# Column vectors loaded as rows, first weights from two queues, two-pass end of the layer norm, softmax sums over two accumulators

## The chip, the core and the metric

The kernel runs on one core of a Trainium2 chip. The metric is the device time of one execution in microseconds (us). TensorE is called PE here, VectorE DVE, ScalarE ACT, GpSimd POOL and SyncE SP, as in the profile.

## The reference

Two layers (D = 1024, 2048 positions, batch 1, float32). Each layer takes shift, scale and gate from `c @ w_ada[l] + b_ada[l]`, normalizes and modulates x, projects it, and runs three mixers on parts of the projection; the merge ends in a second layer norm:

```python
mod = c @ w_ada[l] + b_ada[l]
shift, scale, gate = jnp.split(mod, 3, axis=-1)
h = _layer_norm(x, LN_EPS) * (1.0 + scale[:, None, :]) + shift[:, None, :]
proj = h @ w_in[l]
q, k, v, g_a, cu, cb, cc, g_c, fu, g_f = jnp.split(proj, split_idx, axis=-1)
...
y_attn = _attention(q, k, v) * jax.nn.silu(g_a)
y_conv = cb * _short_conv(cc * cu, conv_w[l]) * jax.nn.silu(g_c)
y_four = _fourier(fu, f_mix[l]) * jax.nn.silu(g_f)
y = jnp.concatenate([y_attn, y_conv, y_four], axis=-1) @ w_out[l]
x = _layer_norm(DEEPNORM_ALPHA * x + (1.0 + gate[:, None, :]) * y, LN_EPS) * ln_g[l] + ln_b[l]
```

Attention has 8 query heads of 64 channels over 2 key heads, softmax over all 2048 positions.

## The kernel before

**Start.** `setup` makes constants and loads c as a tile of 128 partitions x 8 (L96), element by element. `h_norm` loads four tiles of x (L229). `mod_start` (L138) loads b_ada as 128 x 24 in the same manner. `mod_first` (L147, L149) streams eight 256 KB blocks of w_ada for one group of 512 outputs and multiplies them with c on PE; this runs for scale and shift before the first projection. `load_w` (L277) brings blocks of w_in. All loads are issued by SP in program order.

**Attention.** A unit is one chunk of 512 queries and one pair of heads; there are 16 per layer. A unit has four groups (b = 0 to 3) of four key tiles of 128. A group runs, on PE in the order "SSMSMSMM": S is `scores` for one key tile (L903, four terms for two heads into two psA banks), M is `row_max` for a later unit (L829, two matmuls into two psA banks, which DVE reduces at L832). ACT takes the exponential of the scores at L905 into a tile with both heads, tag XA for even key tiles and WL for odd ones, four buffers of each. At the end of the group `weigh` (L916) multiplies the four tiles of the group before with V. The tag psA has seven PSUM banks. At b = 2 `sums` of the unit before comes first (L953): matmuls with ones add up its softmax weights over the keys, four small ones per accumulator, all into one psA bank; ACT copies it (L956). A transposition (L842) and a DVE cast (L844) for the guard rows stand in some groups.

The softmax weights of 16 key tiles are first added up tile by tile. POOL adds most of them at once after the exponential (L938, one add per head); DVE adds four of them after they have been weighed (L935, both heads in one). Which ones is a table:

```python
DVE_KT = (2, 6, 10, 13), range(NKT)
```

The second entry is for the layer's last unit, where DVE adds alone. The first add of an accumulator needs two tiles, so the first tile is held until the second is there. After the last weighing of a unit `add_both` (L944) adds DVE's accumulator to POOL's, on POOL, and `sums` sees one accumulator. In the last unit there is no merge; `sums` runs over the accumulator and two tiles left over. The order on the engines in this part is the order of the program. Fourier mixing runs as background work in the first units of each layer.

**Merge.** `out_proj` multiplies tiles of 128 positions with w_out (L1101 to L1103), DVE adds ALPHA times x (L1132), takes the statistics (L207, L210), POOL takes the reciprocal root (`rsqrt`, L123 and L124), and `finish` ends the layer norm: DVE subtracts the mean and scales (L1070, 1024 wide), DVE multiplies by ln_g (L1073, two halves), POOL adds ln_b (L1074, two halves), and the tile is stored (L1075). `finish` of a tile is issued after the statistics of the next. Between the layers the next layer's normalization and projection are mixed into the last chunk.

Of the kernel before, what the change touches and what calls it, by code (L numbers as in the profile page):

```python
# [10 lines left out]
ALU = mybir.AluOpType  # L11
AX = mybir.AxisListType

P = 128
D = 1024
S = 2048
DEPTH = 2
NB = D // P
HD = 64
CH = 512  # L20
NCH = S // CH
NKT = S // P
# [16 lines left out]
class Trunk:  # L39
# [34 lines left out]
    def setup(self):  # L74
        nc = self.nc
        eye = self.t("HS", [P, P])
        make_identity(nc, eye)
        self.identr = self.const("identr", [P, P], F32R)
        nc.vector.tensor_copy(self.identr, eye)
        self.ident = self.identr.bitcast(F32)  # L80
        self.mhalf = self.const("mhalf", [P, 8])
        nc.gpsimd.memset(self.mhalf, -0.5)
        self.ones = self.const("ones", [P, 32])
        nc.gpsimd.memset(self.ones, 1.0)
        sel = self.t("HS", [P, P])
        nc.gpsimd.memset(sel, 0.0)
        for h in range(2):
            nc.gpsimd.memset(sel[h * HD:h * HD + 1, :], 1.0)
        self.sel = self.const("sel", [P, P], F32R)
        nc.vector.tensor_copy(self.sel, sel)  # L90
        alt = self.const("alt", [P, 2])
        nc.gpsimd.memset(alt[:, 0:1], 1.0)
        nc.gpsimd.memset(alt[:, 1:2], -1.0)
        self.alt = alt.unsqueeze(1).to_broadcast([P, CH // 2, 2])
        self.cT = self.const("cT", [P, NB])
        nc.sync.dma_start(self.cT, self.c[0].rearrange("(b p) -> p b", p=P))  # L96

        self.crep = self.t("TAB", [P, NB, 32])
        nc.vector.tensor_copy(self.crep, self.cT.unsqueeze(2).to_broadcast([P, NB, 32]))

        self.q1 = [self.dram(f"q1_{c}", [P, NPAIR, 2, CH]) for c in range(NCH)]
        self.ga = [[self.dram(f"ga{b}_{c}", [P, CH]) for c in range(NCH)] for b in range(4)]
        self.gf = [[self.dram(f"gf{b}_{c}", [P, CH]) for c in range(NCH)] for b in range(2)]
        self.us = [[self.dram(f"us{b}_{c}", [P, CH]) for c in range(HALF_CH)] for b in range(2)]
        self.fd = [[self.dram(f"fd{b}_{k}", [P, CH]) for k in range(4)] for b in range(2)]
        self.dft = self.dram("dft", [4, 4, 2, P, CH])
        self.yc = [[self.dram(f"yc{b}_{c}", [P, CH]) for c in range(NCH)] for b in range(2)]
        self.yf = [[self.dram(f"yf{b}_{c}", [P, CH]) for c in range(NCH)] for b in range(2)]
        self.gd = [self.dram(f"gd{l}", [D]) for l in range(DEPTH)]
        self.rs_dram = [self.dram(f"rs{i}", [2 * CH]) for i in range(2)]  # L110
        self.rc_dram = [self.dram(f"rc{i}", [2 * CH]) for i in range(2)]
        self.mods = {}
        self.bg = []
        self.gq = []
        self.beside = []
        self.later = []
        self.fu_u = {}
        self.sp2 = {}
        self.x1 = [self.dram(f"x1_{s}", [P, D]) for s in range(NKT)]

    def rsqrt(self, out, var, scale, eps, n):
        nc = self.nc
        nc.gpsimd.tensor_scalar(out, var, scale, eps, ALU.mult, ALU.add)  # L123
        nc.gpsimd.tensor_tensor(out, out, self.mhalf[:, 0:n], ALU.pow)  # L124
# [9 lines left out]

    def mod_start(self, l):
        nc = self.nc
        self.mods[l] = mod = self.small("mod", [P, 3 * NB], bufs=2)
        nc.sync.dma_start(mod, self.b_ada[l].rearrange("(b p) -> p b", p=P))  # L138
        nc.vector.tensor_scalar(mod[:, NB:], mod[:, NB:], 1.0, None, ALU.add)

    def mod_first(self, g, tag="H"):

        nc = self.nc
        ps = self.p("A", (P, P))
        for b in range(NB):
            w = self.t(tag, [P, CH])
            nc.sync.dma_start(w, self.w_ada[0, b * P:(b + 1) * P, g * CH:(g + 1) * CH])  # L147
            for j in range(4):
                nc.tensor.matmul(ps[32 * j:32 * j + 32, :], self.crep[:, b, :], w[:, j * P:(j + 1) * P],  # L149
                                 start=(b == 0), stop=(b == NB - 1))  # L150
        self.mod_add(0, g, self.mod_rows(ps))
# [733 lines left out]
            except StopIteration:  # L885
                self.bg.pop(0)

    DVE_KT = (2, 6, 10, 13), range(NKT)

    def scores(self, u, kt):  # L890
        nc = self.nc
# [27 lines left out]
    def add(self, u, kt, pt, w):  # L919
# [16 lines left out]
        else:  # L936
            for h in range(2):
                self.nc.gpsimd.tensor_tensor(acc[w][:, h], a[:, h], pt[:, h], ALU.add)  # L938

    def add_both(self, u):  # L940

        a, d = u["acc"]["p"], u["acc"].pop("d")
        for h in range(2):
            self.nc.gpsimd.tensor_tensor(a[:, h], a[:, h], d[:, h], ALU.add)  # L944

    def sums(self, u):

# [35 lines left out]
    def attention(self, l):  # L983
        self.yat = {}
        n = len(self.units)
        for g in range((n + 2) * self.NBT):
            ui, b = divmod(g, self.NBT)
            u = self.units[ui] if ui < n else None
# [18 lines left out]
            if 0 < g <= n * self.NBT:  # L1007
                v, c = divmod(g - 1, self.NBT)
                for j in range(self.BATCH):
                    self.weigh(self.units[v], self.BATCH * c + j)  # L1010
                if c == self.NBT - 1 and v < n - 1:
                    self.add_both(self.units[v])
            if u and b == 2:
                u["ga"] = self.t("EV", [P, CH])
                self.nc.sync.dma_start(u["ga"], self.ga[u["pr"]][u["ch"]])
# [37 lines left out]
    def out_proj(self, l):  # L1053
        nc = self.nc
        lnp = {}
# [10 lines left out]
        trans = late = iter(())  # L1066
        tail = []

        def finish(si, xt, mv, rs):
            nc.vector.tensor_scalar(xt, xt, mv[:, 0:1], rs, ALU.subtract, ALU.mult)  # L1070
            for m in range(2):
                xm = xt[:, m * CH:(m + 1) * CH]
                nc.vector.tensor_tensor(xm, xm, lnp["g", m], ALU.mult)  # L1073
                nc.gpsimd.tensor_tensor(xm, xm, lnp["b", m], ALU.add)  # L1074
            nc.sync.dma_start(self.out[0, si * P:(si + 1) * P, :] if l == DEPTH - 1 else self.x1[si], xt)  # L1075

        for ch in range(NCH):
            ys = [self.yat[r, ch] for r in range(4)]
# [12 lines left out]
            for s in range(4):  # L1091
                si = ch * 4 + s
                xt = self.t("XA", [P, D])
# [17 lines left out]
            for n in ((1, 0) if last else (0, 1)):  # L1111
# [9 lines left out]
                for s in range(4):  # L1121
                    si = ch * 4 + s
                    xt = xts[s]
                    if ch:
                        ps = self.p("A")
# [3 lines left out]
                    else:  # L1129
                        ps = pss[s]  # L1130
                    xn = xt[:, n * CH:(n + 1) * CH]
                    nc.vector.scalar_tensor_tensor(xn, xn, ALPHA, ps, ALU.mult, ALU.add)  # L1132
                    if (n == 0) == last:
                        mv = self.small("bmv", [P, 2])
                        rs = self.small("brs", [P, 1])
                        self.row_stats(mv, [xt[:, 0:CH], xt[:, CH:]])
                        self.rsqrt(rs, mv[:, 1:2], 1.0, LN_EPS, 1)
                        if tail:
                            finish(*tail.pop())
                        tail.append((si, xt, mv, rs))  # L1140
                    if last and n:
                        next(trans, None)
                        next(trans, None)
# [2 lines left out]
            if last:  # L1146
                finish(*tail.pop())
# [4 lines left out]
    def run(self, layers=DEPTH):  # L1152
# [1 line left out]
        self.setup()  # L1154
        xs = self.h_norm(0, 0)
        self.mod_start(0)
        self.mod_first(2)
        self.mod_first(0)
        w_fu = self.load_w(0, COL_FU, 0)
        h0 = [], []  # L1160
        self.chan_first(h0, self.h_trans_steps(0, xs, *h0), w_fu, self.spill(self.us, AF.Copy),
# [2 lines left out]
        w = self.load_w(0, COL_KV, P)  # L1164
# [78 lines left out]
```

## Time and profile before

| | us |
|---|---|
| three runs | 2670.92, 2672.66, 2678.76 |
| median | 2672.66 |
| profiled execution, its own time | 2675.07 |
| span of its instructions | 2673.2 |
| PE busy | 2623.7 |
| DVE busy | 1791.0 |
| POOL busy | 1191.6 |
| ACT busy | 904.5 |

The profile is of one execution, the one of 2675.07 us; its trace starts at 0 and ends at 2673.2. The mean clock granted to PE was 0.994 of full speed. Matmuls are pipelined and their ends are modelled, so PE's busy time is an upper view, and starts are more exact than ends.

### The profile page before, as it was taken

What the parts mean: (1) busy time and instruction counts of PE and PEld (TensorE: products, weight loads), DVE (VectorE), ACT (ScalarE), POOL (GpSimd) and SP (SyncE); (2) the same over time, 40 slices, a digit from 0 to 9 for tenths busy, and PEclk for the clock granted to TensorE, in tenths of its full rate; (3) what the DMA queues carried; (4) which work ended last, traced back from release to release, by engine and by line L of the source; (5) the groups of instructions that cost most, each with busy time, mean ns of one, the idle gap of its engine ahead of it and who ended that gap; (6) DMA issues with size and microseconds to landing.
All of it is one profiled execution on the core that took longest, in us unless ns stands there. A gap on an engine that the chain in (4) does not pass through costs nothing.

```text
span 2673.2 us, 39706 instructions
## 1 busy us (share of the span) xinstructions
PE 2623.7 (98%) x14820; PEld 1838.7 (69%) x14820; DVE 1791.0 (67%) x3053; ACT 904.5 (34%) x1789; POOL 1191.6 (45%) x989
## 2 busy tenths in 40 slices
PE   7999999999999999999999999999999999999998
PEld 5888888765555555568888888887655555555786
DVE  6754773457778877787885347535577877787755
ACT  3321521134444454530232125211444445445200
POOL 1200020046789888814231001100677898887134
PEclk9999999999999999999999999999999999999999
DMA  9753462322211111045445222522322110111432
GB/s 303 231 166 107 133 184 71 106 96 83 92 53 60 41 41 37 21 140 180 140 138 173 52 99 72 162 78 76 110 95 77 57 56 30 32 37 45 147 114 95
DMA packets 198673, 269.11 MB, mean 101 GB/s; under 512 B 38352, under 2 KB 109392, under 8 KB 197968
## 3 DMA queue, kind: packets, MB, share of 16 engines
q1 hardware_dynamic: 198480, 266.58, 31.3%
q8 instruction: 116, 1.90, 0.3%
q14 instruction: 77, 0.63, 0.1%
HBM read 205.29 MB, written 69.48 MB: 103 GB/s over the span
## 4 chain that ended last, share of the span: by engine, by line
PE 91%; DVE 4%; DMA 2%; issue 1%; POOL 1%; ACT 1%; SPq 0%; POOLq 0%; DVEq 0%; ACTq 0%
PE psA L903 19%; PE psC L916 16%; PE psA L372 9%; PE psA L373 9%; PE psA L374 9%; PE psA L829 5%; PE psA L1101 4%; PE psA L1103 4%; PE psA L1102 4%; PE psA L320 2%; PE psA L322 2%; PE psA L321 2%; DVE mx L832 1%; PE psA L953 1%; PE psA L749 1%
## 5 line engine op out<-in xcount | busy, mean ns | idle before, releaser
L832 DVE TENSOR_REDUCE mx<-psA 128x1 f32<-128x512 f32 x1024 | 634.0, 682 | 216.5 <-PE psA L829 215.4
L938 POOL TENSOR_TENSOR WH<-WH,WL 128x512 f32<-128x512 f32 x360 | 488.4, 1383 | 44.3 <-ACT WL L905 44.2
L903 PE MATMUL psA<-TAB,KK 64*128 64x512 f32 x3072 | 471.7, 409 | 5.7 <-DVE HS L844 5.4
L905 ACT ACTIVATE XA<-psA 128x512 f32<-128x512 f32 x512 | 278.7, 598 | 448.4 <-PE psA L903 326.9
L372 PE MATMUL psA<-H,WH 128*128 128x512 f32 x1008 | 399.1, 396 | 0.0
L373 PE MATMUL psA<-H,WH 128*128 128x512 f32 x1008 | 393.6, 390 | 0.0
L374 PE MATMUL psA<-H,WL 128*128 128x512 f32 x1008 | 392.9, 390 | 0.0
L903 PEld LDWEIGHTS psA<-TAB,KK 64*128 64x128 f32 x3072 | 274.7, 185 | 143.6 <-issue 51.1
L938 POOL TENSOR_TENSOR WH<-WH,XA 128x512 f32<-128x512 f32 x240 | 306.9, 1305 | 57.5 <-ACT XA L905 57.5
L905 ACT ACTIVATE WL<-psA 128x512 f32<-128x512 f32 x512 | 279.8, 606 | 23.1 <-PE psA L903 21.2
L916 PE MATMUL psC<-XA,V 128*64 128x512 f32 x1024 | 270.3, 606 | 0.0
L938 POOL TENSOR_TENSOR WH<-XA,WL 128x512 f32<-128x512 f32 x60 | 76.0, 1287 | 426.2 <-DVE mx L832 376.3
L916 PE MATMUL psC<-WL,V 128*64 128x512 f32 x1024 | 263.1, 592 | 0.0
L132 DVE TENSOR_TENSOR WL<-WR,WH 128x512 fp32r<-128x512 f32 (+2 forms) x240 | 113.3, 508 | 164.4 <-ACT WH L129 163.8
L372 PEld LDWEIGHTS psA<-H,WH 128*128 128x128 f32 x1008 | 189.2, 188 | 48.5 <-issue 9.3
L374 PEld LDWEIGHTS psA<-H,WL 128*128 128x128 f32 x1008 | 189.2, 188 | 40.3
L829 PE MATMUL psA<-KK,TAB 64*128 64x512 f32 x1024 | 208.1, 403 | 8.0 <-DVE mx L832 5.7
L373 PEld LDWEIGHTS psA<-H,WH 128*128 128x128 f32 x1008 | 189.4, 188 | 37.1
L903 PE MATMUL psA<-QS,sel 64*128 64x512 f32 x1024 | 206.2, 390 | 0.0
L129 ACT ACTIVATE WH<-WR 128x512 fp32r<-128x512 f32 (+2 forms) x248 | 107.8, 487 | 261.7 <-PE psA L373 111.8
L916 PEld LDWEIGHTS psC<-WL,V 128*64 128x64 f32 x1024 | 73.6, 137 | 146.7 <-issue 146.7
L123 POOL TENSOR_SCALAR rq<-rq 128x8 f32<-128x8 f32 (+1 forms) x48 | 10.6, 220 | 321.0 <-DVE rq L432 279.3
(237 smaller groups left out, 4101.9 us busy)
## 6 DMA issues: line engine op xcount, KB each, us to landing
WR<-in_w_in SPq DMA_DIRECT2D x176, 256.0 KB
WR<-in_w_ada SPq DMA_DIRECT2D x64, 256.0 KB
q<-EV SPq DMA_DIRECT2D x64, 256.0 KB
TAB<-q SPq DMA_DIRECT2D x64, 256.0 KB
H<-dft SPq DMA_DIRECT2D x64, 256.0 KB
XA<-in_x SPq DMA_DIRECT2D x24, 512.0 KB
XA<-x SPq DMA_DIRECT2D x20, 512.0 KB
dft<-in_k_dft SPq DMA_DIRECT2D x32, 256.0 KB
```

What stands on the lines that cost most here:

```text
L129: nc.scalar.activation(hi, src, AF.Copy)
L132: (lo_eng or nc.vector).tensor_tensor(lo, src, hi.bitcast(F32), ALU.subtract)
L372: nc.tensor.matmul(ps, w1, hh[b], start=(b == 0), stop=False)
L373: nc.tensor.matmul(ps, w1, hl[b], start=False, stop=False)
L374: nc.tensor.matmul(ps, w2, hh[b], start=False, stop=(b == NB - 1))
L829: nc.tensor.matmul(pss[h], u["q"][0][r, s * P:(s + 1) * P], self.kk1[u["kv"]][kc][r], start=True, stop=True)
L832: nc.vector.tensor_reduce(out=u["mx"][h][:, s, kc:kc + 1], in_=pss[h], axis=AX.X, op=ALU.max)
L903: nc.tensor.matmul(pss[h], k[r], q[r], start=i == 0, stop=i == len(terms) - 1)
L905: nc.scalar.activation(pt[:, h, :], pss[h], AF.Exp, scale=HD ** -0.5)
L916: nc.tensor.matmul(u["pv"][h * HD:(h + 1) * HD, :], v, pt[:, h, :], start=(kt == 0), stop=(kt == NKT - 1))
L938: self.nc.gpsimd.tensor_tensor(acc[w][:, h], a[:, h], pt[:, h], ALU.add)
L1101: nc.tensor.matmul(ps, yh[:, sl], wh, start=first, stop=False)
```

## The change

`columns` loads c and b_ada as 8 and 24 rows of 128 elements, transposes them on PE and copies them from PSUM. `mod_first` can issue every second block of w_ada from ACT's queue; the first two groups do. DVE adds key tiles 3, 7, 11 and 15, `add_both` is gone, and `sums` runs over both accumulators. `finish` is split: `centre` computes (x - mean) * ln_g in one DVE pass per half, before the root is there, `finish` times the root plus ln_b in a second pass; the very last tile is stored in halves.

```diff
@@ -92,8 +92,7 @@
         nc.gpsimd.memset(alt[:, 0:1], 1.0)
         nc.gpsimd.memset(alt[:, 1:2], -1.0)
         self.alt = alt.unsqueeze(1).to_broadcast([P, CH // 2, 2])
-        self.cT = self.const("cT", [P, NB])
-        nc.sync.dma_start(self.cT, self.c[0].rearrange("(b p) -> p b", p=P))
+        self.cT = self.columns(self.const("cT", [P, NB]), self.c[0], nc.sync)
 
         self.crep = self.t("TAB", [P, NB, 32])
         nc.vector.tensor_copy(self.crep, self.cT.unsqueeze(2).to_broadcast([P, NB, 32]))
@@ -118,6 +117,17 @@
         self.sp2 = {}
         self.x1 = [self.dram(f"x1_{s}", [P, D]) for s in range(NKT)]
 
+    def columns(self, out, src, queue):
+
+        nc = self.nc
+        n = out.shape[1]
+        rows = self.t("HS", [n, P])
+        queue.dma_start(rows, src.rearrange("(b p) -> b p", p=P))
+        ps = self.p("A", (P, n))
+        nc.tensor.transpose(out=ps, in_=rows, identity=self.ident[0:n, 0:n])
+        nc.vector.tensor_copy(out, ps)
+        return out
+
     def rsqrt(self, out, var, scale, eps, n):
         nc = self.nc
         nc.gpsimd.tensor_scalar(out, var, scale, eps, ALU.mult, ALU.add)
@@ -134,17 +144,17 @@
 
     def mod_start(self, l):
         nc = self.nc
-        self.mods[l] = mod = self.small("mod", [P, 3 * NB], bufs=2)
-        nc.sync.dma_start(mod, self.b_ada[l].rearrange("(b p) -> p b", p=P))
+        self.mods[l] = mod = self.columns(self.small("mod", [P, 3 * NB], bufs=2), self.b_ada[l], nc.sync)
         nc.vector.tensor_scalar(mod[:, NB:], mod[:, NB:], 1.0, None, ALU.add)
 
-    def mod_first(self, g, tag="H"):
+    def mod_first(self, g, tag="H", queues=1):
 
         nc = self.nc
         ps = self.p("A", (P, P))
         for b in range(NB):
             w = self.t(tag, [P, CH])
-            nc.sync.dma_start(w, self.w_ada[0, b * P:(b + 1) * P, g * CH:(g + 1) * CH])
+            queue = nc.scalar if b % queues else nc.sync
+            queue.dma_start(w, self.w_ada[0, b * P:(b + 1) * P, g * CH:(g + 1) * CH])
             for j in range(4):
                 nc.tensor.matmul(ps[32 * j:32 * j + 32, :], self.crep[:, b, :], w[:, j * P:(j + 1) * P],
                                  start=(b == 0), stop=(b == NB - 1))
@@ -885,7 +895,7 @@
             except StopIteration:
                 self.bg.pop(0)
 
-    DVE_KT = (2, 6, 10, 13), range(NKT)
+    DVE_KT = (3, 7, 11, 15), range(NKT)
 
     def scores(self, u, kt):
         nc = self.nc
@@ -936,12 +946,6 @@
         else:
             for h in range(2):
                 self.nc.gpsimd.tensor_tensor(acc[w][:, h], a[:, h], pt[:, h], ALU.add)
-
-    def add_both(self, u):
-
-        a, d = u["acc"]["p"], u["acc"].pop("d")
-        for h in range(2):
-            self.nc.gpsimd.tensor_tensor(a[:, h], a[:, h], d[:, h], ALU.add)
 
     def sums(self, u):
 
@@ -1008,8 +1012,6 @@
                 v, c = divmod(g - 1, self.NBT)
                 for j in range(self.BATCH):
                     self.weigh(self.units[v], self.BATCH * c + j)
-                if c == self.NBT - 1 and v < n - 1:
-                    self.add_both(self.units[v])
             if u and b == 2:
                 u["ga"] = self.t("EV", [P, CH])
                 self.nc.sync.dma_start(u["ga"], self.ga[u["pr"]][u["ch"]])
@@ -1066,13 +1068,20 @@
         trans = late = iter(())
         tail = []
 
-        def finish(si, xt, mv, rs):
-            nc.vector.tensor_scalar(xt, xt, mv[:, 0:1], rs, ALU.subtract, ALU.mult)
+        def centre(xt, mv):
             for m in range(2):
                 xm = xt[:, m * CH:(m + 1) * CH]
-                nc.vector.tensor_tensor(xm, xm, lnp["g", m], ALU.mult)
-                nc.gpsimd.tensor_tensor(xm, xm, lnp["b", m], ALU.add)
-            nc.sync.dma_start(self.out[0, si * P:(si + 1) * P, :] if l == DEPTH - 1 else self.x1[si], xt)
+                nc.vector.scalar_tensor_tensor(xm, xm, mv[:, 0:1], lnp["g", m], ALU.subtract, ALU.mult)
+
+        def finish(si, xt, rs):
+            dst = self.out[0, si * P:(si + 1) * P, :] if l == DEPTH - 1 else self.x1[si]
+            for m in range(2):
+                sl = slice(m * CH, (m + 1) * CH)
+                nc.vector.scalar_tensor_tensor(xt[:, sl], xt[:, sl], rs, lnp["b", m], ALU.mult, ALU.add)
+                if si == NKT - 1:
+                    nc.sync.dma_start(dst[:, sl], xt[:, sl])
+            if si < NKT - 1:
+                nc.sync.dma_start(dst, xt)
 
         for ch in range(NCH):
             ys = [self.yat[r, ch] for r in range(4)]
@@ -1137,7 +1146,8 @@
                         self.rsqrt(rs, mv[:, 1:2], 1.0, LN_EPS, 1)
                         if tail:
                             finish(*tail.pop())
-                        tail.append((si, xt, mv, rs))
+                        centre(xt, mv)
+                        tail.append((si, xt, rs))
                     if last and n:
                         next(trans, None)
                         next(trans, None)
@@ -1154,8 +1164,8 @@
         self.setup()
         xs = self.h_norm(0, 0)
         self.mod_start(0)
-        self.mod_first(2)
-        self.mod_first(0)
+        self.mod_first(2, queues=2)
+        self.mod_first(0, queues=2)
         w_fu = self.load_w(0, COL_FU, 0)
         h0 = [], []
         self.chan_first(h0, self.h_trans_steps(0, xs, *h0), w_fu, self.spill(self.us, AF.Copy),
```

In the built program PE's order is the same in attention apart from the added sums, but what its matmuls wait for moves. At the end of the group that follows the sums, in a steady unit, these are the last four row-max matmuls (into psA) and the first weighing (into psC); the name in brackets is the engine whose progress is waited for. Before:

```order
L829 MATMUL psA_1947_9479<-KK_528_3036,TAB_1878_9201 128x512 [waits DVE_49]
L829 MATMUL psA_1948_9480<-KK_528_3036,TAB_1878_9201 128x512 [waits DVE_49]
L829 MATMUL psA_1949_9485<-KK_573_3265,TAB_1878_9201 128x512 [waits DVE_49]
L829 MATMUL psA_1950_9486<-KK_573_3265,TAB_1878_9201 128x512 [waits DVE_49]
L916 MATMUL psC_1927_9390<-XA_1907_9306,V_186_996 64x512 x2
```

and with the change:

```order
L839 MATMUL psA_2250_10736<-KK_534_3048,TAB_2181_10456 128x512 [waits DVE_49]
L839 MATMUL psA_2251_10737<-KK_534_3048,TAB_2181_10456 128x512 [waits Activation_49]
L839 MATMUL psA_2252_10742<-KK_579_3277,TAB_2181_10456 128x512 [waits Activation_49]
L839 MATMUL psA_2253_10743<-KK_579_3277,TAB_2181_10456 128x512 [waits DVE_49]
L926 MATMUL psC_2230_10643<-XA_2210_10559,V_192_1008 64x512 x2
```

The second and third now wait for ACT (an exponential that has emptied a bank) where all four waited for DVE (a maximum that has emptied one).

SP's queue at the start, loads in the order of issue (mod is b_ada's tile, cT is c's). Before:

```order
L96 DMA cT<-in_c 128x8x1
L229 DMA XA_167<-in_x 128x1024
L229 DMA XA_173<-in_x 128x1024
L229 DMA XA_179<-in_x 128x1024
L229 DMA XA_185<-in_x 128x1024
L138 DMA mod_202<-in_b_ada 128x24x1
L147 DMA H_206<-in_w_ada 128x512
L147 DMA H_212<-in_w_ada 128x512
L147 DMA H_218<-in_w_ada 128x512
```

and with the change:

```order
L239 DMA XA_171<-in_x 128x1024
L125 DMA HS_84<-in_c 8x128
L239 DMA XA_177<-in_x 128x1024
L239 DMA XA_183<-in_x 128x1024
L239 DMA XA_189<-in_x 128x1024
L157 DMA H_214<-in_w_ada 128x512
L157 DMA H_226<-in_w_ada 128x512
L125 DMA HS_207<-in_b_ada 24x128
L157 DMA H_238<-in_w_ada 128x512
```

The tile of x is now first, c and b_ada come as rows, b_ada behind two blocks of weights. Every second block of w_ada has gone to ACT's queue, here the last three of its eight and what follows them:

```order
L157 DMA H_286<-in_w_ada 128x512
L157 DMA H_298<-in_w_ada 128x512
L157 DMA H_310<-in_w_ada 128x512
L165 ACT_TABLE_LOAD
L165 ACTIVATE HS_262<-psA_213 128x128
L139 ACTIVATE WH_321<-WR_323 128x512
```

ACT's loads stand ahead of its table load and its first copy.

DVE at the very end, the last tile of the last layer. Before:

```order
L1132 SCALAR_TENSOR_TENSOR XA_25598<-XA_25598,psA_25824 128x512 [waits PE_49]
L207 BN_STATS bst_25852<-XA_25598 128x6 [waits DVE_49]
L210 BN_AGGR bmv_25850<-bst_25852 128x2 [waits DVE_49]
L1070 TENSOR_SCALAR XA_25598<-XA_25598,bmv_25850,brs_25851 128x1024 [waits DVE_49,Pool_49]
L1073 TENSOR_TENSOR XA_25598<-XA_25598,TAB_24602 128x512 [waits DVE_49]
L1073 TENSOR_TENSOR XA_25598<-XA_25598,TAB_24604 128x512
```

and with the change:

```order
L1141 SCALAR_TENSOR_TENSOR XA_25646<-XA_25646,psA_25869 128x512 [waits PE_49]
L217 BN_STATS bst_25897<-XA_25646 128x6 [waits DVE_49]
L220 BN_AGGR bmv_25895<-bst_25897 128x2 [waits DVE_49]
L1074 SCALAR_TENSOR_TENSOR XA_25646<-XA_25646,bmv_25895,TAB_24659 128x512 [waits DVE_49]
L1074 SCALAR_TENSOR_TENSOR XA_25646<-XA_25646,bmv_25895,TAB_24661 128x512
L1080 SCALAR_TENSOR_TENSOR XA_25646<-XA_25646,brs_25896,TAB_24663 128x512 [waits DVE_49,Pool_49]
L1080 SCALAR_TENSOR_TENSOR XA_25646<-XA_25646,brs_25896,TAB_24665 128x512 [waits DVE_49]
```

The wait for POOL (the root) has moved from the first pass after the statistics to the third, and POOL's two adds behind the last row are gone.

## Rows read from the trace of the kernel before

**Rows 1.** page, busy time of PE: us, share, instructions

```profile
PE 2623.7 (98%) x14820; PEld 1838.7 (69%) x14820; DVE 1791.0 (67%) x3053; ACT 904.5 (34%) x1789; POOL 1191.6 (45%) x989
```

**Rows 2.** waits of PE: us in total, times, longest

```profile
PE psA L829 <- DVE mx L832: 5.7, 28, 0.5
PE psA L903 <- DVE HS L844: 5.4, 2, 2.7
PE psA L349 <- DVE H L131: 4.0, 1, 4.0
```

**Rows 3.** timeline of PE, two groups of one unit: start us, us, what

```profile
941.65 0.96 PE L903 MATMUL psA<-TAB,KK 64*128 64x512 f32 x6
...
946.08 0.98 PE L829 MATMUL psA<-KK,TAB 64*128 64x512 f32 x3
...
947.68 1.08 PE L916 MATMUL psC<-XA,V 128*64 128x512 f32 x4
...
951.42 0.96 PE L903 MATMUL psA<-TAB,KK 64*128 64x512 f32 x6
...
955.79 0.63 PE L829 MATMUL psA<-KK,TAB 64*128 64x512 f32 x4
956.35 1.08 PE L916 MATMUL psC<-XA,V 128*64 128x512 f32 x4
...
959.94 0.96 PE L903 MATMUL psA<-TAB,KK 64*128 64x512 f32 x6
```

**Rows 4.** timeline of ACT, the same unit: start us, us, what, idle before

```profile
948.87 1.08 ACT L905 ACTIVATE XA<-psA 128x512 f32<-128x512 f32 x2 [3.87 <-PE psC L916]
```

**Rows 5.** timeline of DVE, the same unit

```profile
944.03 4.96 DVE L832 TENSOR_REDUCE mx<-psA 128x1 f32<-128x512 f32 x8 [3.97 <-PE psA L829]
```

**Rows 6.** timeline of PE, sums of a layer's last unit, second and third accumulator

```profile
1172.12 0.61 PE L953 MATMUL psA<-XA,ones 128*32 128x256 f32 x8
1172.55 0.61 PE L953 MATMUL psA<-WL,ones 128*32 128x256 f32 x8
```

**Rows 7.** windows at the start: us, busy by engine, PEclk, DMA share, GB/s

```profile
8.00:11.00 3.00, 0.00 (x0) 0.00 (x0) 2.96 (x9) 0.00 (x0) 0.00 (x0) 1.00 0.92 95
11.00:25.00 14.00, 10.38 (x134) 4.76 (x134) 4.54 (x14) 1.32 (x4) 1.23 (x2) 0.98 1.03 364
```

**Rows 8.** chain that ended last, its pieces at the start: start us, us

```profile
3.80 5.67 SPq L147
```

**Rows 9.** timeline of DVE between the layers

```profile
1360.40 0.81 DVE L1070 TENSOR_SCALAR XA<-XA,bmv,brs 128x1024 f32<-128x1024 f32 x1 [0.72 <-POOL brs L124]
1361.25 1.29 DVE L1073 TENSOR_TENSOR XA<-XA,TAB 128x512 f32<-128x512 f32 x2
...
1368.09 0.42 DVE L132 TENSOR_TENSOR XA<-WR,XA 128x256 fp32r<-128x256 f32 x1 [1.28 <-DMA x<-XA]
```

**Rows 10.** groups of DVE by line: busy us, mean ns, idle before

```profile
L528 DVE SCALAR_TENSOR_TENSOR QS<-EV,cw,QS 128x511 f32<-128x511 f32 x16 | 11.9, 747 | 0.1
```

**Rows 11.** timeline of DVE at the end

```profile
2663.39 0.21 DVE L210 BATCH_NORM_AGGREGATE bmv<-bst 128x2 f32<-128x12 f32 x1
2665.07 0.81 DVE L1070 TENSOR_SCALAR XA<-XA,bmv,brs 128x1024 f32<-128x1024 f32 x1 [1.48 <-POOL brs L124]
```

**Rows 12.** timeline of POOL at the end

```profile
2666.69 2.86 POOL L1074 TENSOR_TENSOR XA<-XA,TAB 128x512 f32<-128x512 f32 x2 [1.65 <-DVE XA L1073]
```

**Rows 13.** groups of DVE by line, first adds of accumulators

```profile
L935 DVE TENSOR_TENSOR WH<-XA,XA 128x1024 f32<-128x1024 f32 x30 | 52.8, 1760 | 0.0
```

**Rows 14.** timeline of DVE, one long add

```profile
798.88 7.26 DVE L935 TENSOR_TENSOR WH<-XA,XA 128x1024 f32<-128x1024 f32 x1
```

**Rows 15.** timeline of POOL beside it

```profile
798.85 4.99 POOL L938 TENSOR_TENSOR WH<-WH,WL 128x512 f32<-128x512 f32 x4
```

**Rows 16.** timeline of PE, the group after it and the next group's start

```profile
801.40 0.96 PE L903 MATMUL psA<-TAB,KK 64*128 64x512 f32 x6
...
815.92 0.96 PE L903 MATMUL psA<-TAB,KK 64*128 64x512 f32 x6
```

## The prediction

> **What bounds the kernel now.** I read the busy times first: TensorE (PE) is busy for 98% of the span [rows 1], so time is won only where a matmul goes away or a gap between matmuls closes, and any matmul added is paid in full. Then the waits of PE by releaser [rows 2]: they add up to little, but the ends of matmuls are modelled, so a wait shorter than the modelled end doesn't show its length. I therefore measured attention from start to start in PE's timeline. Sixteen units per layer each run four groups (scores, row maxima for a later unit, then the weighted sums of the group before). The group right after the softmax sums (the "sums group", b = 2) is slow: its last four row-max matmuls start at 946.08 and the weighing at 947.68, 1.60 us later; in the next group the same takes 955.79 to 956.35, 0.56 us [rows 3]. So 1.04 us is lost. From the first score matmul to the next group's the two take 9.77 and 8.52 us [rows 3]. The waits view counts this place 28 times (row-max matmul on VectorE's maxima, 5.7 us in its reckoning) [rows 2]. By start times it is 28 x 1.04 = 29.1 us.
>
> Why it waits: in that group ScalarE sits idle for 3.87 us, until the weighing matmul, before an exponential into an XA tile at 948.87 [rows 4]. That is key tile 10. Even key tiles use XA, four buffers; tiles 2 and 6 are VectorE's and both are held until its first add, which needs the two of them and stands behind the group's maxima; 8 is in use; 4 comes free only when it is weighed at the group's end. The scores of tiles 10 and 11 meanwhile keep four of the seven psA banks, and the last row-max matmuls must take turns on the others, each behind a reduction on VectorE, which gives eight in 4.96 us, 0.62 each [rows 5].
>
> **The change, part by part.** *Which tiles VectorE adds.* Now 3, 7, 11, 15, all in WL. Tile 10 finds the XA buffer of tile 2, which was weighed a group earlier, so its exponential is no longer late; only tile 11 (WL) still waits for a weighing. In the order of the built program the last four row-max matmuls of the sums group wait for VectorE, ScalarE, ScalarE, VectorE, the pattern of the groups that lose nothing, where before all four waited for VectorE. I take the whole loss as gone: -29.1 us. The other end, nothing gained, is the second rival.
>
> *No merge of accumulators.* GpSimd loses two adds per unit; PE did not wait for them except through the sums, so I cost that at nothing. PE gains four small matmuls per unit. Their price stands where three accumulators are already summed, in the last unit: the second starts at 1172.12, the third at 1172.55, 0.43 us [rows 6]. 15 units x 2 layers x 0.43 = +12.9 us, on a packed PE, so all of it counts. Since what follows on PE is moved by the same 0.43 us, VectorE and GpSimd only get more room.
>
> *Start.* The first 39 us are a chain of loads. From 8 to 11 us the 16 DMA engines are 0.92 busy but move 95 GB/s, against 364 GB/s between 11 and 25 us [rows 7]: 3 x (1 - 95/364) = 2.2 us of loading lost, where the bias vector is loaded as 3072 single elements; the issue behind it waits 5.67 us [rows 8]. The 1024 elements of c should cost a third of that, an estimate of 0.7 us. Loaded as rows of 512 bytes both go away: -2.9 us. The two transposes and copies that replace them are short and lie under the load of x and the first weights. Issuing eight of the first weights from ScalarE's queue I cost at nothing: between 11 and 25 us the DMA engines are already full (share 1.03) [rows 7], so earlier issues only queue. Three more 256 KB blocks of w_in now pass ahead of the last eight w_ada blocks, 0.79 MB at 364 GB/s = 2.2 us; their own matmuls fill that time. Ends: -0.7 (those 2.2 us count) and -5.7 (the whole blocked issue was on the chain).
>
> *End of the layer norm, between the layers.* PE waits 4.0 us once for a VectorE cast [rows 2]. VectorE works in order, and ahead of that cast it waited 0.72 us for GpSimd's reciprocal root and 1.28 us for the store of the last tile [rows 9]. Now centring comes before the root is needed, and the store no longer waits for GpSimd's two bias adds. Against 2.0 us of waits stand four passes of 0.75 us (the mean of the same kind of pass with both inputs in SBUF) [rows 10], 3.0, in place of 0.81 + 1.29 = 2.1 [rows 9]: +0.9. Net -1.1. Ends: +0.9 (the waits only move) and -2.0. In the other tiles PE has matmuls of its own, which cover VectorE's 0.9 us; without that cover it would be 0.9 us in some 30 tiles.
>
> *Tail.* The last statistics end at 2663.39 + 0.21 = 2663.60; GpSimd is still in the adds of the tile before, VectorE waits 1.48 us for the root [rows 11], and GpSimd's adds end at 2666.69 + 2.86 = 2669.55 [rows 12]. Now: four passes of 0.75 from 2663.60, with the root done under the first two, end at 2666.60, 2.95 us earlier. The last store is half as large: 0.26 MB at 364 GB/s would be 0.7 us less; as the first half may still be in the queue I take half of it. -3.3 in all; ends -2.6 and -3.7.
>
> **Sum.** -29.1 + 12.9 - 2.9 - 1.1 - 3.3 = -23.5 us against the profiled execution's 2675.07: 2651.6. That execution was 2.4 us over the median shown (2672.66), so the forecast is **2649 us**. Its parts' ends give 2645 to 2654, apart from what follows.
>
> **Rivals.** *First, slower: VectorE's add is held by GpSimd.* VectorE's first adds of a unit take 1.76 us in the mean of 30 [rows 13], but the one at 798.88 took 7.26 us [rows 14], while GpSimd's adds ran on without a break, four of them from 798.85 in 4.99 us [rows 15]. The transpose cast behind it came late, and the PE group from 801.40 to 815.92 took 14.52 us, 6.0 more than 8.52 [rows 3, 16]. The waits view has two such cases (score matmul on that cast) [rows 2]. After the change GpSimd adds three key tiles in a row, six adds, between VectorE's, so runs are longer, and as every unit keeps the same cadence a bad coincidence would come back in each. Four more cases (4 x 6.0 = 24.0) eat the whole gain; six more give 2649 + 36 = 2685; one in each of 28 units 2817. Against it: only two of those 30 adds were held so, and GpSimd loses two operations per unit. And the two cases may go away: 2649 - 12 = 2637. As the trace has two such cases already, I give this rival 0.12, half of it with six more cases or above.
>
> The Trainium skill, page "SBUF — State Buffer", section "Who interferes with whom", has a rule for this pair: a VectorE instruction with two SBUF inputs and a GpSimd instruction that reads SBUF exclude each other for one whole instruction, and who starts first decides. By that rule an add of VectorE waits for one GpSimd add at most, this rival can't occur, and the time stays at the forecast. The trace agrees with it for the mean of 1.76 us [rows 13] and not at 798.88, where 7.26 us hold several GpSimd adds [rows 14, 15]; the measurement decides.
>
> *Second: the stall stays in another form.* Tile 11's scores still hold two banks until the weighing, and the sums group could wait there instead. Then the 29.1 us are not won and the 12.9 are paid: 2649 + 29 = 2678, no change that can be measured. Half of it left: 2664. For it: VectorE's eight maxima take 4.96 us in either case [rows 5]; against it the waits named above. 0.12, two thirds of it at the full price.
>
> *Third: the vectors or the tail do nothing* (another load is the last one): at most 7 us, 2656, inside the range.
>
> **How the numbers follow.** A measurement here can tell about 0.3%, 8 us, from no change: faster is under 2664.6, slower over 2680.7. Forecast 0.73, the first rival 0.12, the second 0.12, 0.03 for what I have not seen. Faster: 0.73, a quarter of the first (0.03), a sixth of the second (0.02): 0.78. Same: 0.03 + 0.09 + 0.02 = 0.14. Slower: 0.06 + 0.01 + 0.01 = 0.08. The range is 2636 (both held cases gone) to 2666 (half of the stall left, or three more held cases); outside lie the slower cases, the full second rival, and little below.
>
> **What would show it.** Right: waits of row-max matmuls on maxima gone, the sums group at about 8.7 us beside 8.5, sums 0.43 us longer each, a unit 0.6 us shorter, no slice of 95 GB/s near 8 us, the last VectorE pass near 3 us after the last statistics, no GpSimd adds behind it. Wrong: VectorE's adds of 5 us or more in more than two places, PE waits on the transpose cast, a sums group still at 9.7 us, or score matmuls that wait for the exponential of tile 11.

## The result and the profile after

The changed kernel takes 2638.67 us (median of four runs, 2637.78 to 2639.83) against 2672.78 us: a ratio of 0.9863, 95% interval 0.9851 to 0.9876, so 34 us less. The forecast was 2649 us in a range from 2636 to 2666. The profiled execution took 2638.81 us, its span is 2637.0 us.

The page of the changed kernel, its span and the busy times:

```profile
span 2637.0 us, 40062 instructions
...
PE 2605.5 (99%) x15063; PEld 1833.3 (70%) x15063; DVE 1773.7 (67%) x3088; ACT 908.1 (34%) x1789; POOL 1054.1 (40%) x865
```

PE is still the bound [rows 1]. It is busy for 18 us less although it has more matmuls. The reason is in how a page counts: the ends of matmuls are modelled, so part of a stall counts as busy time, and the 1024 row-max matmuls alone fall from 208.1 to 185.5 us.

The spans differ by 36.2 us. The starts of the first and last score matmuls (L903 before, L913 after) give the stages:

| stage | before, us | after, us | difference | forecast |
|---|---|---|---|---|
| to the first score matmul | 564.62 | 566.10 | +1.5 | -2.9 |
| scores of layer 0, first to last | 599.18 | 585.42 | -13.8 | |
| scores of layer 1, first to last | 598.14 | 584.92 | -13.2 | |
| both | | | -27.0 | -29.1 + 12.9 = -16.2 |
| between the two (merge, next projection) | 716.23 | 709.28 | -7.0 | -1.1 |
| from the last score matmul to the end | 195.03 | 191.28 | -3.8 | -3.3 |

The waits of PE in the changed kernel:

```profile
PE psA L127 <- DVE identr L79: 8.9, 1, 8.9
PE psC L267 <- ACT HS L269: 3.3, 4, 2.0
PE psA L172 <- ACT HS L165: 3.1, 4, 2.0
PE psA L127 <- DMA HS<-in_b_ada: 2.9, 1, 2.9
PE psA L361 <- DVE H L142: 1.4, 3, 0.6
```

All three rows of [rows 2] are gone: the 28 waits of row-max matmuls on maxima, the two of score matmuls behind a late cast, and the 4.0 us between the layers. The first four rows stand in the first 70 us, and two of them are new (L127, the transposes of the vectors); the last is three short waits, later on.

PE's timeline in one unit, the group with the sums before it and the next group's start:

```profile
931.10 1.07 PE L957 MATMUL psA<-WH,ones 128*32 128x256 f32 x16
932.10 0.97 PE L913 MATMUL psA<-TAB,KK 64*128 64x512 f32 x6
...
936.53 0.62 PE L839 MATMUL psA<-KK,TAB 64*128 64x512 f32 x4
...
937.08 1.08 PE L926 MATMUL psC<-XA,V 128*64 128x512 f32 x4
...
940.82 0.96 PE L913 MATMUL psA<-TAB,KK 64*128 64x512 f32 x6
```

The last row maxima to the weighing: 936.53 to 937.08, 0.55 us, where the sums group had 1.60 [rows 3]. The sums take 1.00 us (931.10 to 932.10), 0.43 more than with one accumulator, as forecast. ACT shows why in the same group:

```profile
933.39 1.09 ACT L915 ACTIVATE XA<-psA 128x512 f32<-128x512 f32 x2 [0.77 <-PE psA L913]
934.36 1.09 ACT L915 ACTIVATE WL<-psA 128x512 f32<-128x512 f32 x2
935.48 1.09 ACT L915 ACTIVATE XA<-psA 128x512 f32<-128x512 f32 x2
939.13 1.09 ACT L915 ACTIVATE WL<-psA 128x512 f32<-128x512 f32 x2 [2.56 <-POOL WH L948]
```

Tile 10 (third row) follows at once, where it stood 3.87 us late [rows 4]. Tile 11 is late now, by 2.56 us, and costs PE nothing; the profile names a GpSimd add as what it waited for.

The end, DVE and then POOL:

```profile
2630.36 0.21 DVE L220 BATCH_NORM_AGGREGATE bmv<-bst 128x2 f32<-128x12 f32 x1
2630.60 1.41 DVE L1074 SCALAR_TENSOR_TENSOR XA<-XA,bmv,TAB 128x512 f32<-128x512 f32 x2
2632.46 1.41 DVE L1080 SCALAR_TENSOR_TENSOR XA<-XA,brs,TAB 128x512 f32<-128x512 f32 x2 [0.44 <-POOL brs L134]
```

```profile
2630.65 0.75 POOL L133 TENSOR_SCALAR brs<-bmv 128x1 f32<-128x1 f32 x1 [3.21 <-DVE bmv L220]
2631.48 0.94 POOL L134 TENSOR_TENSOR brs<-brs,mhalf 128x1 f32<-128x1 f32 x1
```

From the last statistics' start to the last pass it is 3.5 us (2630.36 to 2633.87), against 6.2 us to the end of POOL's adds [rows 11, 12]. The root is not quite covered: POOL's two steps, 0.74 us before, take 1.69 us beside DVE's two centring passes, which take 1.41.

### The profile page after: what moved, and what is told of

It reads as the page before. It is cut to its first block, busy times and chain, and to the rows that moved or that the text cites. A ratio compares the mean times of both kernels' runs of the same rounds, so it can differ in the third digit from the quotient of the medians.

```text
span 2637.0 us, 40062 instructions
## 1 busy us (share of the span) xinstructions
PE 2605.5 (99%) x15063; PEld 1833.3 (70%) x15063; DVE 1773.7 (67%) x3088; ACT 908.1 (34%) x1789; POOL 1054.1 (40%) x865
## 4 chain that ended last, share of the span: by engine, by line
PE 95%; DVE 2%; DMA 2%; ACT 1%; POOL 0%; issue 0%; SPq 0%; POOLq 0%; DVEq 0%; ACTq 0%
PE psA L913 19%; PE psC L926 17%; PE psA L382 9%; PE psA L383 9%; PE psA L384 9%; PE psA L839 5%; PE psA L1110 4%; PE psA L1112 4%; PE psA L1111 4%; PE psA L330 2%; PE psA L332 2%; PE psA L331 2%; PE psA L957 1%; PE psA L361 1%; PE psA L359 1%; PE psA L759 1%
## 5 line engine op out<-in xcount | busy, mean ns | idle before, releaser
L948 POOL TENSOR_TENSOR WH<-WH,XA 128x512 f32<-128x512 f32 x420 | 595.6, 1439 | 157.6 <-ACT XA L915 157.6
L913 PE MATMUL psA<-TAB,KK 64*128 64x512 f32 x3072 | 469.2, 407 | 0.3
L913 PEld LDWEIGHTS psA<-TAB,KK 64*128 64x128 f32 x3072 | 273.0, 184 | 136.9 <-issue 51.9
L948 POOL TENSOR_TENSOR WH<-XA,WL 128x512 f32<-128x512 f32 x60 | 75.8, 1284 | 422.4 <-DVE mx L842 376.3
L948 POOL TENSOR_TENSOR WH<-WH,WL 128x512 f32<-128x512 f32 x180 | 228.6, 1290 | 0.0
L913 PE MATMUL psA<-QS,sel 64*128 64x512 f32 x1024 | 205.1, 389 | 0.4 <-DMA QS<-HS 0.4
L839 PE MATMUL psA<-KK,TAB 64*128 64x512 f32 x1024 | 185.5, 396 | 0.0
L133 POOL TENSOR_SCALAR brs<-bmv 128x1 f32<-128x1 f32 x32 | 19.4, 607 | 365.1 <-DVE bmv L220 365.0
```

The costliest lines, as they stand in the source:

```text
L839: nc.tensor.matmul(pss[h], u["q"][0][r, s * P:(s + 1) * P], self.kk1[u["kv"]][kc][r], start=True, stop=True)
L913: nc.tensor.matmul(pss[h], k[r], q[r], start=i == 0, stop=i == len(terms) - 1)
```

## The experiments

Two theories stood after the comparison. *Mine:* the held tile makes the 28 stalls, and GpSimd's lighter load in the units with Fourier gate multiplies freed the two long VectorE adds. *Its rival:* the merge on GpSimd makes both, and the table of tiles is of no matter. The table of measured times (each beside runs of the kernel before on the same chip) comes first, then what each run was for.

| run | us | before there | first score matmul | long adds (over 3 us) | sums group |
|---|---|---|---|---|---|
| 1 table only | 2666.78 (2655.69 to 2668.35) | 2676.57 | 563.5 | 3 | 8.7 |
| 2 no merge only | 2677.03 | 2676.57 | 564.8 | 0 | 9.8 |
| 3 layer norm only | 2665.18 | 2676.57 | 564.6 | 2 | 9.8 |
| 4 start only | 2675.42 | 2676.57 | 566.3 | 2 | 9.8 |
| 5 tiles 2, 7, 11, 15 | 2668.44 | 2673.87 | 567.0 | 0 | 9.8 |
| 6 gate on VectorE | 2668.97 | 2673.87 | 563.9 | 0 | 9.8 |
| 7 merge, gate on VectorE | 2632.94 | 2673.87 | 566.8 | 0 | 8.7 |
| 8 rows only | 2677.33 (one) | 2673.87 | 567.3 | 2 | 9.8 |
| 9 queues only | 2679.57 (one) | 2673.51 | 567.5 | 2 | 9.8 |
| 10 rows in EV | 2678.83 (one) | 2673.51 | 568.7 | 2 | 9.8 |
| 11 merge where room | 2627.86 | 2673.51 | 563.8 | 0 | 8.7 |
| 12 and rows for layer 0 | 2629.26 (2626.90 to 2631.51) | 2672.34 | 560.3 | 1 | 8.7 |

The last three columns are from each run's trace; the sums group is PE's start to start, in us.

**1. Only the table.**

```diff
-    DVE_KT = (2, 6, 10, 13), range(NKT)
+    DVE_KT = (3, 7, 11, 15), range(NKT)
```

> The kernel before with only the table of VectorE's key tiles changed to 3, 7, 11, 15; the merge on GpSimd stays. If the held tile 2 makes the stall: 28 x 1.04 us are gone and no matmul is added, 2672.8 - 29.1 = 2643.7 us, or down to 2633 if the two long VectorE adds go away as well (6.0 and 5.1 us); the sums groups take 8.7 us. If the merge on GpSimd is what delays those groups: 2672 to 2674 us and sums groups of 9.8 us.

Measured 2666.78 us, a ratio of 0.9956 (0.9938 to 0.9974). The sums groups are at 8.7 us, so the stall does hang on the table. But the time is far above 2643.7: three VectorE adds are held, two at great cost. DVE, POOL and PE around the first of the costly ones:

```profile
2092.43 9.67 DVE L935 TENSOR_TENSOR WH<-WL,WL 128x1024 f32<-128x1024 f32 x1
```

```profile
2089.91 2.49 POOL L938 TENSOR_TENSOR WH<-WH,XA 128x512 f32<-128x512 f32 x2
2092.37 2.52 POOL L938 TENSOR_TENSOR WH<-WH,WL 128x512 f32<-128x512 f32 x2
2094.85 2.50 POOL L938 TENSOR_TENSOR WH<-WH,XA 128x512 f32<-128x512 f32 x2
2097.33 1.25 POOL L780 TENSOR_TENSOR H<-H,H 128x512 f32<-128x512 f32 x1
2098.55 2.47 POOL L938 TENSOR_TENSOR WH<-WH,XA 128x512 f32<-128x512 f32 x2
2102.93 2.51 POOL L938 TENSOR_TENSOR WH<-WH,WL 128x512 f32<-128x512 f32 x2 [1.92 <-ACT WL L905]
```

```profile
2102.42 1.65 PE L903 MATMUL psA<-TAB,KK 64*128 64x512 f32 x5 [5.95 <-DVE HS L844]
```

POOL has no idle time until 2101.0, and VectorE's add ends just after that, at 2102.1: it got in when POOL ran dry (nothing was left that it could start). PE waits 5.95 us for the cast behind it, and the group takes 16.5 us. This is the first rival of the prediction, brought on by the table with the merge left in. The executions spread over 12.7 us; that the number of held adds changes from one to the next would explain it, but only the profiled one, the fastest of the six, has a trace. In its first layer a late GpSimd costs PE time without a held add: the group from 802.50 takes 12.35 us where its like take 8.57. PE waits there for a small load (QS) that SP issued late, behind the store of a gate multiply that GpSimd had finished late:

```profile
805.15 1.20 PE L903 MATMUL psA<-QS,sel 64*128 64x512 f32 x2 [1.68 <-DMA QS<-HS]
```

**2. Only the merge taken out.**

```diff
-                if c == self.NBT - 1 and v < n - 1:
-                    self.add_both(self.units[v])
```

> The kernel before with only the merge taken out; VectorE keeps tiles 2, 6, 10, 13. If the held tile makes the stall: it stays, and 30 x 0.43 us are paid: 2672.8 + 12.9 = 2685.7 us (6 us more or less for each long VectorE add that comes or goes). If the merge makes the stall: 2672.8 - 29.1 + 12.9 = 2656.6 us.

Measured a ratio of 1.0007 (0.9998 to 1.0017): no change. The stalls stay, and both long adds are gone. The waits of PE and the groups of DVE in this run:

```profile
PE psA L829 <- DVE mx L832: 5.7, 28, 0.5
```

```profile
L935 DVE TENSOR_TENSOR WH<-XA,XA 128x1024 f32<-128x1024 f32 x30 | 38.2, 1275 | 0.0
```

The 28 waits stand as before [rows 2]; the adds that took 1.76 us in the mean [rows 13] take 1.28. Paid are 12.9 us, won back some 11 (6.0 and 5.1 us, the two groups' excess before). So the merge does not make the stall, and without its two adds per unit no VectorE add is held in this trace.

**3. Only the end of the layer norm**, `centre`, `finish` and the halved last store, as in the change's diff.

> The kernel before with only the two-pass end of the layer norm and the halved last store. If the 6.4 us gained between the layers belong to it: 2672.8 - 6.4 - 3.2 = 2663.2 us, and no wait of 4 us between the layers. If that gain came from the rest of the change (another state of the loads or of GpSimd at that place), only the tail is left: 2669.6 us with the wait still there.

Measured a ratio of 0.9957 (0.9942 to 0.9971), 11.4 us less than before there, with 9.6 expected. The 4 us wait is gone, so the gain between the layers belongs to this part. PE's order there (585 matmuls from 1284 us on) is the same in both traces. What went away are waits of VectorE for roots and stores, here from 1322 us to the cast that PE waited for in the kernel before, then over the like stretch of this run (from 1319 us):

```profile
DVE XA L1070 <- POOL brs L124: 3.0, 3, 1.3
DVE XA L132 <- DMA x<-XA: 2.5, 2, 1.3
...
DVE XA L1078 <- POOL brs L124: 1.3, 3, 0.4
```

Three waits for a root and two for a store made 5.5 us; in this run three waits for a root make 1.3 us. Windows of the kernel before around that wait, then of this run at the same times:

```profile
1368.00:1372.00 4.00, 0.02 (x1) 0.02 (x1) 3.91 (x13) 0.00 (x0) 0.57 (x2) 1.00 0.28 68
1372.00:1376.00 4.00, 3.56 (x17) 3.08 (x18) 3.97 (x12) 1.44 (x3) 0.80 (x1) 0.58 0.21 64
1376.00:1380.00 4.00, 4.00 (x22) 4.00 (x23) 3.41 (x6) 1.18 (x3) 0.00 (x0) 0.57 0.33 76
```

```profile
1368.00:1372.00 4.00, 4.00 (x34) 4.00 (x35) 3.93 (x9) 1.61 (x5) 0.00 (x0) 1.00 0.21 64
1372.00:1376.00 4.00, 4.00 (x36) 4.00 (x35) 3.89 (x8) 0.66 (x2) 0.46 (x2) 1.00 0.86 249
```

The columns are as in [rows 7]. Before, PE stood still for 4 us and then ran at a granted clock of 0.58 and 0.57 for 8 us: for most of that time on the lower of its two levels (1.2 of 2.4 GHz). The stall cost the wait and some 3 us behind it.

**4. Only the start.**

> The kernel before with only the start changed: c and b_ada as rows, transposed, first weights from two queues. If the start costs what the two traces show at the first score matmul, 1.5 us: 2674.3 us, first score matmul near 566.1 us. If that loss came from another part's influence on the order, the forecast of -2.9 us should show: 2669.9 us, first score matmul near 561.7 us.

Measured a ratio of 0.9998 (0.9988 to 1.0007). The first score matmul comes at 566.3 us: the start loses 1.6 us on its own.

**5. Which held tile.** `DVE_KT = (2, 7, 11, 15)` in the changed kernel.

> The changed kernel with VectorE's key tiles 2, 7, 11, 15, so that only the first of them lies in XA. If the stall hangs on tile 2 alone (it holds the XA buffer that tile 10's exponential needs; tile 6 would be unweighed anyway): sums groups of 9.8 us again, 2638.7 + 28 x 1.04 = 2667.8 us. If it takes two held tiles in one pool of four: 2638.7 us, sums groups of 8.7 us.

Measured 2668.44 us, within 1 us of the first case. Tile 2 alone makes the stall; tile 6 never mattered, since in that group it is not weighed yet whoever adds it. ACT's timeline has the old row back:

```profile
949.70 1.09 ACT L915 ACTIVATE XA<-psA 128x512 f32<-128x512 f32 x2 [3.87 <-PE psC L926]
```

**6. The gate multiplies off GpSimd.**

```diff
-            nc.gpsimd.tensor_tensor(y[b][c], y[b][c], g, ALU.mult)
+            nc.vector.tensor_tensor(y[b][c], y[b][c], g, ALU.mult)
```

> The kernel before with the eight gate multiplies per layer of the Fourier part on VectorE in place of GpSimd. If VectorE's adds of over 7 us come from a GpSimd that has no idle time in the units with those multiplies: both are gone, 11 us less than before (2676.6 on this chip), 2665.6 us. If they come from the mere meeting of an add with GpSimd's adds: they stay, the time is that of before or up to 3 us more for the longer VectorE.

Both long adds are gone. The time fell by 4.9 us and not by 11: in four groups the multiply on VectorE delays the maxima, and PE waits again (score matmuls on maxima). Such a group takes 10.24 us in place of 9.14, and the one before it 0.3 to 0.5 us more, 6 us for the four:

```profile
PE psA L903 <- DVE mx L832: 2.2, 4, 0.6
```

**7. The change with the merge back**, and the gate multiplies on VectorE.

> The changed kernel with the merge on GpSimd back, so that the sums run over one accumulator, and the gate multiplies on VectorE. If the merge harms only where GpSimd has no idle time beside it: no VectorE add over 3 us, 30 x 0.43 us less, 2638.7 - 12.9 = 2625.8 us. If the merge harms in itself: adds over 3 us in other units, 2639 us or more.

Measured 2632.94 us. No add is held; the four delayed groups are here too, and make some 6 of the 7.1 us above 2625.8.

**8 to 10. What the start loses.** Run 8 has the rows alone, run 9 the second queue alone; run 10 is run 8 with the rows in another tile:

```diff
-        rows = self.t("HS", [n, P])
+        rows = self.t("EV", [n, P])
```

> The kernel before with only c and b_ada loaded as rows and transposed, all weights from one queue. If the rows lose the time at the start (their transposes stand ahead of PE's first matmuls and wait): first score matmul 1.5 us later than before's 564.6 us. If the second queue loses it: 2.9 us earlier, 561.7 us.

> The kernel before with only every second block of the first two groups of w_ada issued from ScalarE's queue; c and b_ada load element by element as before. If the loads are bound by the DMA engines: first score matmul within 0.5 us of before's 564.6 us. If the earlier issue wins the slice in which single elements were moved: 2 us earlier, 562.6 us. If the queues share badly: later than 566 us.

> As the run with rows alone (first score matmul 567.3 us), but the rows land in a tile of the tag EV in place of HS, so that SP's load of b_ada needs not wait until VectorE has freed an HS tile at 8.5 us. If that wait in SP's queue is what costs: 564.6 us or less. If the order of the work on PE and VectorE after 40 us costs, which the transposes have moved: 567 us as before, with PE busy under 17 of the 20 us from 40 to 60.

All three reach the first score matmul late, by 2.7, 2.9 and 4.1 us, each in one execution. In run 10 SP is not held at b_ada, the DMA engines are full from 8 to 11 us, and still it is the latest. Its windows from 8 us, and PE near 50 us:

```profile
8.00:11.00 3.00, 1.24 (x18) 0.95 (x18) 3.00 (x11) 0.00 (x0) 0.00 (x0) 1.00 1.04 392
...
40.00:60.00 20.00, 14.91 (x74) 11.77 (x73) 16.39 (x42) 6.64 (x11) 1.28 (x2) 0.83 0.71 227
```

```profile
47.90 0.40 PE L403 MATMUL psA<-H,WL 128*128 128x512 f32 x1
50.75 0.30 PE L266 MATMUL psC<-identr,KK 128*128 128x128 f32 x1 [2.45 <-DVE KK L246]
...
53.40 0.47 PE L266 MATMUL psC<-identr,KK 128*128 128x128 f32 x1 [0.44 <-DVE KK L246]
53.80 0.30 PE L127 MATMUL psA<-identr,EV 24*128 24x24 f32 x1
54.03 0.58 PE L358 MATMUL psA<-WH,H 128*128 128x256 f32 x1
```

At 47.90 this run is ahead of the kernel before by 3 us; then PE stands behind the transposes of the second chunk's x (L266), which wait for VectorE, and the key and value projection (L358 to L360) behind them. In the kernel before 35 of these matmuls come first in PE's order and fill the wait; the transposition of the second layer's b_ada (L127 at 53.80) has moved them in the built program, and in that of the change too. From 50 us on the clock falls too, 0.83 in the mean of the window. So the loads do come earlier, as forecast, and the order gives it back. In run 9 those 35 matmuls still come first; there ScalarE's order has moved, and its copy for a transpose on PE stands behind splits of w_in that wait for their load. PE's wait for that copy in run 9, ScalarE's wait ahead of it, and the same wait of PE in the kernel before:

```profile
26.69 0.48 PE L163 MATMUL psA<-identr,HS 128*128 128x128 f32 x1 [3.72 <-ACT HS L156]
...
23.98 1.34 ACT L129 ACTIVATE WH<-WR 128x512 fp32r<-128x512 f32 x2 [4.79 <-DMA WR<-in_w_in]
...
24.19 0.35 PE L162 MATMUL psA<-identr,HS 128*128 128x128 f32 x1 [0.40 <-ACT HS L155]
```

In the changed kernel the like wait is 1.98 us. How much of run 9's 2.9 us this makes is not shown.

**11. The merge where there is room**, with the old start: the merge is left out for units 3 to 6 alone.

> The changed kernel with the old start, the merge back except in units 3 to 6 of each layer (those next to the gate multiplies, which stay on GpSimd). If the merge harms only there: 22 x 0.43 = 9.5 us and 1.5 us of the start less than the change, 2638.7 - 11.0 = 2627.7 us, no VectorE add over 3 us. If adds are held elsewhere: 6 us more for each.

Measured 2627.86 us, ratio 0.9832 (0.9816 to 0.9849), within 0.2 us of the first case: faster than both kernels.

**12. And rows for the first layer only**, the second layer's b_ada element by element:

```diff
+        if l == 0:
+            self.columns(mod, self.b_ada[l], nc.sync)
+        else:
+            nc.sync.dma_start(mod, self.b_ada[l].rearrange("(b p) -> p b", p=P))
```

> The run with the merge where there is room (2627.9 us, first score matmul at 563.8 us), plus c and the first layer's b_ada as rows through EV tiles; the second layer's b_ada loads element by element as in the kernel before, so that no transposition of it stands in PE's order near 54 us. In the built program the transposes of the second chunk then stand behind 35 matmuls of the first key and value projection again, as before the change, where with rows for both layers they stand ahead of them. If that order is what the start lost: the 2.9 us of the loads show, first score matmul near 560.9 us, 2625.0 us. If the rows lose time by themselves: first score matmul at 564 us or later, 2628 us or more.

The first score matmul comes at 560.3 us, 4.3 us before the kernel before and 3.5 before run 11, and the 35 matmuls come first again: the order was what the rows lost at the start. The median is 2629.26 us all the same, and the 2625.0 was not reached. In the profiled execution (2631.35 us) one VectorE add took 7.71 us and its group 14.5, 6 us too long; two of the four runs are at 2627, and have no trace.

## Why the prediction was right, and where it was not

The direction and the main mechanism held. *Stall of the sums group:* forecast 28 x 1.04 us gone; the groups fell from 9.77 to 8.72 us, 1.05 us each; runs 1 and 5 show that the table does it. One part of the reason was wrong: I named tiles 2 and 6 as holding the buffers; it is tile 2 alone (run 5). *Sums:* 0.43 us per unit, as measured.

*First rival.* I saw the two held adds and kept them in the forecast, as the only thing that could turn the sum. They went away, 11 us, and that is the end I had priced at 2637 without a chance of its own. That the total came so near to this end is luck: what was won beyond the forecast between the layers (5.9 us) and what the start lost of it (4.4 us) nearly cancel.

What I had wrong is the condition. I feared longer runs of adds; what the held cases have in common is a GpSimd that had run without idle time for 15 us or more, and an add that got in only when it ran dry. In the unit of each layer with most gate multiplies GpSimd had 24 adds and four multiplies of about 1.25 us, 35 us in a unit of 36; now 26 of them, 32.5 in 35.4. Each VectorE add that gets in costs GpSimd about 1 us more (two adds in 3.50 us beside one, in 2.50 without), and there are three in a unit. By this estimate GpSimd had 38 us of work in 36, and now has 35.5 in 35.4. So it is still full, and yet no add is held: the unit with four multiplies in the changed kernel, its busy times (POOL 35.22 of 35.39 us), two rows of POOL and the three adds of VectorE:

```profile
788.90:824.29 35.39, 35.39 (x244) 19.25 (x242) 29.33 (x42) 17.86 (x34) 35.22 (x27) 1.00 0.22 69
...
794.42 2.50 POOL L948 TENSOR_TENSOR WH<-WH,WL 128x512 f32<-128x512 f32 x2
796.88 3.50 POOL L948 TENSOR_TENSOR WH<-WH,XA 128x512 f32<-128x512 f32 x2
...
797.15 2.08 DVE L945 TENSOR_TENSOR WH<-WL,WL 128x1024 f32<-128x1024 f32 x1
805.83 1.83 DVE L945 TENSOR_TENSOR WH<-WH,WL 128x1024 f32<-128x1024 f32 x1
814.41 2.13 DVE L945 TENSOR_TENSOR WH<-WH,WL 128x1024 f32<-128x1024 f32 x1
```

A GpSimd without idle time is therefore not enough to hold an add. What the traces show is how often it happens: all seven that have both the merge and GpSimd's multiplies in that unit (the kernel before, runs 1, 3, 4, 8, 9 and 10) have two held adds or more; of the seven that lack one of the two there, six have none. The seventh, run 12, has one, in the next unit, which has multiplies and no merge. Why one add is held and another not stays open.

*Between the layers:* the term of -1.1 was mis-sized; it is -7.0 (run 3 alone: -7.7). I had set the added passes against the waits of one tile, 0.72 and 1.28 us; the tiles ahead of it had such waits too, 5.5 us in all, of which 4.2 went away (run 3). Part of the rest is that VectorE's instructions beside POOL's bias adds were slow: the cast at 1363.29 took 0.70 us then and a like one 0.43 in run 3. PE's wait went altogether, and with it the half clock behind it. *Start:* the step that failed is that the transposes that replace the single elements "lie under the load of x and the first weights", and with it -2.9. I had counted two; the third, of the second layer's b_ada, stands near 51 us and came with another order on PE, and +1.5 was measured. I had looked at the queues' order and not at PE's beyond 40 us. *Tail:* -3.3 forecast; span minus the start of PE's last matmul gives 11.7 us before and 8.5 after, -3.2. *The second queue*, costed at nothing, moved ScalarE's order; alone it reached the first score matmul 2.9 us later (run 9, one execution).

The Trainium skill's rule (page "SBUF — State Buffer", section "Who interferes with whom") that one of the two engines shuts the other out for one whole instruction fits most adds here, which take up to 2.4 us. It does not fit the held ones: 7.26 us before and 9.67 us in run 1, during which four and six GpSimd instructions started.

## What to carry to other kernels

Look at which buffer a slow consumer holds, not only at how much it does: moving VectorE's first held tile from one pool to the other was worth 30 us here (run 5) with no less work. Before giving a helper engine more to do, add up its load in the fullest stretch, with what another engine's instructions cost it there: with some 38 us of work in a unit of 36, single VectorE waits of about 1 us turned into 6. And where a scheduler orders the program, read the order of the bounding engine again after moving a load, since a transposition may move what fills its waits.

## What was not expected of the hardware

VectorE's add of two SBUF tiles takes 1.2 us alone. Beside GpSimd's adds it shows two outcomes over all fourteen traces: up to 2.4 us, where it gets in after the GpSimd add that runs, or 7.1 to 9.8 us (15 adds), until GpSimd runs dry: each of the 15 ends some 1.08 us after the last GpSimd instruction that passed it (one of 3.78 us in run 1 lies between). Its start alone does not tell which: 13 of the 15 had started within 0.19 us after a GpSimd instruction's start, but so had 26 others that got in after it, and two held ones had started after 0.51 and 0.81 us. And a PE wait of 4 us was followed by 8 us near half clock (0.58 and 0.57 in the kernel before), so that it cost nearly twice its length.
